# A two-block network on one core: the recurrence's preparation starts at the second product instead of the first, and activations move by 32 bytes

## The chip, the cores and the metric

The kernel runs on one core of one Trainium2 chip. The metric is the device time of one execution in microseconds. TensorE is called PE below, VectorE DVE, ScalarE ACT, GpSimd POOL and SyncE SP.

## The reference, cut to what matters

Two residual blocks of width 2048 run over 256 tokens. Each is a mixer followed by a sparse "peer" feed-forward layer, and everything is float32:

```python
# block 1
merged = gate_a * (o_a @ w_branch_a) + gate_b * (o_b @ w_branch_b)
x = x + merged @ w_out                                  # out_proj
x = x + peer(rmsnorm(x))                                # peer layer 1
...
# block 2: an mLSTM and an S5 recurrence in parallel, then
x = x + merged2 @ w_out_2
x = x + peer(rmsnorm(x))                                # peer layer 2

def peer(xb):            # 16384 experts, 8 heads x 16 chosen per token
...
    a = gelu(u_emb[expert] . xb)
    return sum((g * a) * v_emb[expert])

def s5_groups(u, lam_re, lam_im, log_dt, b_re, b_im, c_re, c_im, d, glu_w):
    dt = exp(log_dt);  mag = exp(lam_re * dt)
    ar = mag * cos(lam_im * dt);  ai = mag * sin(lam_im * dt)
...                                       # powers of ar + i*ai, b and c scaled by them
```

The part of S5 that depends on parameters alone (the powers, and the tables made from them) can be computed at any time before block 2. It is called S5's preparation below.

## The kernel before, in words

**Products.** A float32 product is made of three products of halves (`products`, matmul at L220): hi·hi, hi·lo and lo·hi. Weights come in tiles of 128x2048, in two parts `w_raw` of 128x1024, by DMAs from SP. For each part ACT writes `w_hi` (L205), and DVE (L211) or POOL (L209) writes `w_lo`. Each of these names has four buffers, so two tiles.

**The peer layer** does not gather experts. In each of two rounds (r = 0, 1) the first product `u` multiplies the tokens with 64 weight tiles (128x256 outputs, 48 matmuls per tile, operands `hT_hi` and `hT_lo`); Gelu and a gate follow, and the second product `v` uses 64 weight tiles again (512 columns, 24 matmuls a tile, operands `coef_hi` and `coef_lo`, made on ACT and DVE at L260).

**The gates of a round** are prepared in 32 groups of 8 tokens. For each group POOL and DVE make one-hot matrices `oh1` (L491; 6 of 8 on POOL in round 0, `G0 = 6`), DVE makes `oh`, `rh` and `rl` (L494 to L499), and PE multiplies them into `ps_g` (L505, L506).

**Order.** Work beside the main loop is written as generators ("lanes") in `K.bg`; `K.step(n)` runs them for n credits between weight tiles. The order inside each engine is then settled when the program is built: an instruction that is ready by the builder's own estimate may be placed ahead of earlier-written ones, unless `behind(x)` holds it until after x. Engines execute their own rows in order.

**S5's preparation** (`_s5_prepare`, L1094) is such a lane, run within peer layer 1. Its first part is about 215 small DVE instructions, mostly on 128x32, two Sin activations, and the table `base`. POOL then makes eight tables from `base` (L1194 to L1196, six instructions of 128x256 and two DMAs, L1201 and L1202, each). Then eight blocks follow (`expand`): DVE makes `s_work` (L1212 to L1219) in the buffer where `base` was, PE transposes it and multiplies (L1244, L1249: 192 matmuls in all), POOL expands a second table, and POOL's DMAs write both to DRAM.

**Addresses.** `hT()` allocates the two halves of the transposed activations. In the program's memory map they stand 32 bytes past a multiple of 64 bytes; weight parts and `coef` stand at a multiple of 64; the attention output `o` and the normalised `cqT` of block 1 also stand at a multiple of 64. So the two operands of a matmul differ by 32 bytes (modulo 64) wherever `hT` is used, and by 0 for `coef`, `o` and `cqT`. `out_proj` takes its activations in an `hT()` as well, with the weights as the moving operand (512 columns, 384 matmuls in each of the two blocks).

Of the kernel before, what the change touches and what calls it, by code (L numbers as in the profile page):

```python
# [7 lines left out]
F32, F32R, F16, U32, I32 = dt.float32, dt.float32r, dt.float16, dt.uint32, dt.int32  # L8
AF = mybir.ActivationFunctionType
OP = mybir.AluOpType  # L10
AX = mybir.AxisListType

P = 128
T = 256
TB = 2
D = 2048
KD = D // P
# [16 lines left out]
class Ctx:  # L34


    def __init__(self, ctx, tc):
        self.tc, self.nc = tc, tc.nc
        nc = self.nc
        pool = lambda name, bufs, **kw: ctx.enter_context(tc.tile_pool(name=name, bufs=bufs, **kw))  # L40
        self.const = pool("const", 1)
        self.small = pool("small", 1)
        self.state = pool("state", 1)
        self.wp = pool("weights", 2)
        self.pad = pool("pad", 1)
        self.two = pool("pairs", 2)
        self.pad3 = pool("pad3", 1, side="right")
        self.top = pool("hT", 1, side="right")
        for p, n in ((self.pad, 0), (self.pad3, 448)):
            if n:  # L50
                nc.gpsimd.memset(p.tile([P, n // 4], F32, name="pad"), 0.0)
        self.ps = pool("psum", 2, space=bass.MemoryType.PSUM)
        it = self.const.tile([P, P], F32, name="iota_f")
        nc.gpsimd.iota(it, pattern=[[1, P]], base=0, channel_multiplier=-1,
                       allow_small_or_imprecise_dtypes=True)
        self.diff = it
        self.ident = self.const.tile([P, P], F32, name="ident")
        nc.vector.tensor_scalar(self.ident, it, 0.0, None, op0=OP.is_equal)
        self.iota = self.const.tile([P, P], F16, name="iota_h")
        nc.gpsimd.iota(self.iota, pattern=[[1, P]], base=0, channel_multiplier=0,  # L60
                       allow_small_or_imprecise_dtypes=True)
        self.half_pi = self.const.tile([P, 1], F32, name="half_pi")
        nc.vector.memset(self.half_pi, float(np.pi / 2))
        self.x = self.state.tile([P, TB, D], F32, name="x")
        self.sq = self.small.tile([P, TB, 4], F32, name="x_sq")
        self.sq2 = self.small.tile([P, TB, 4], F32, name="x_sq2")
        self.twice, self.first, self.normed, self.done, self.fused = False, {}, {}, set(), {}
        self.bg = []
        self.late = []
        self.credit = 0.0  # L70
        self.fine = 0
        self.last = None

    def defer(self, fn):

# [75 lines left out]
    def step(self, n):  # L151
# [4 lines left out]
        while self.credit > 0 and idle < len(self.bg):  # L156
# [6 lines left out]
            self.credit -= took  # L163
            idle = 0 if took else idle + 1

    def lane(self):

        chain = []

        def run():  # L170
            while True:
                while not chain:
                    yield 0
                x = chain.pop(0)
                if x is None:
                    return
                yield from x

        self.bg.append(run())
        return chain  # L180
# [15 lines left out]
    def weights_now(self, src, n, pool):  # L196
        nc = self.nc
        self.fine -= 1
        h = n // 2
        raw, hi, lo = ([self.wp.tile([P, D // 2], d, name=nm, bufs=4)[:, :h] for _ in range(2)]  # L200
                       for nm, d in (("w_raw", F32), ("w_hi", F32R), ("w_lo", F32R)))
# [4 lines left out]
        for i in range(2):  # L206
            m = max(0, min(h, (2 - i) * h - pool))
            if m < h:
                nc.gpsimd.tensor_tensor(lo[i][:, m:], raw[i][:, m:], hi[i][:, m:].bitcast(F32), op=OP.subtract)  # L209
            if m:  # L210
                nc.vector.tensor_tensor(lo[i][:, :m], raw[i][:, :m], hi[i][:, :m].bitcast(F32), op=OP.subtract)  # L211
        return Halves(hi, h), Halves(lo, h)

    def products(self, items, left, half=None):
# [66 lines left out]
            self.last = v.scalar_tensor_tensor(r, q, 1.5, r, op0=OP.add, op1=OP.mult)  # L281
        return r

    def hT(self):
        return (self.top.tile([P, KD, T], F32R, name="hT_hi"),
                self.top.tile([P, KD, T], F32R, name="hT_lo"))

    def norm_T(self):

# [38 lines left out]
def peer(K, wq, keys, u, v, g_out, g_next=None, dst=None, later=None):  # L328
# [8 lines left out]
    nc, ctx = K.nc, ExitStack()  # L337
# [144 lines left out]
    TG = 8  # L482
    st = {}

    def gates(r, on_pool):

        def prepare(t0):
            oh1 = K.two.tile([P, TG, P], F16, name="oh1", tag="two_a", bufs=2)
            for t in range(TG):
                e = nc.gpsimd if t < on_pool else nc.vector  # L490
                e.tensor_scalar(oh1[:, t], K.iota, i1T[:, t0 + t:t0 + t + 1], None, op0=OP.is_equal)  # L491
            oh2 = rp.tile([P, TG, NJ], F16, name="oh2", bufs=2)
            b2 = lambda a: a[:, t0:t0 + TG, None].to_broadcast([P, TG, NJ])
            nc.vector.tensor_tensor(oh2, K.iota[:, None, r * NJ:(r + 1) * NJ].to_broadcast([P, TG, NJ]),  # L494
# [40 lines left out]
    for r in range(2):  # L535
        st.update(done=0, groups=0, A=[rp.tile([P, 16, T], F32, name="acts", tag="acts", bufs=4) for _ in range(4)])
        K.bg.append(gates(r, 8 if r else G0))
        for jp in range(NJ // 2):
            if r == 0 and st["groups"] == T // TG and later is not None:
                K.bg.append(later(rp))  # L540
                later = None
            ps = K.ps.tile([P, 2, T], F32, name="ps_u", bufs=2)
            for jj in range(2):
                if jp == NJ // 2 - 1 and jj:
# [13 lines left out]
            K.credit = 0.0  # L558
            K.step(1)
        if later is not None:  # L560
            K.bg.append(later(rp))
            later = None
        end = r == 1
        ext = {}
# [118 lines left out]
def mix1(K, I):  # L683
# [6 lines left out]
    ps_u = lambda shape: K.ps.tile(shape, F32, name="ps_u", bufs=2)  # L690
    ps_v = lambda shape: K.ps.tile(shape, F32, name="ps_v", bufs=4)

    grow = b8([P, D], "gain_row")[0:1]
    nc.sync.dma_start(grow, I["norm_mix_row"])
    ones = wt([P, T], "ones", 3, tag="one")[0:1, 0:P]
# [299 lines left out]
    for i in range(KD):  # L995
# [7 lines left out]
        nc.vector.tensor_tensor(m, m, ps[:, 0], op=OP.mult)  # L1003
        nc.vector.tensor_tensor(g1, g1, ps[:, 1], op=OP.mult)
        nc.vector.tensor_tensor(m, m, g1, op=OP.add)
    mh, ml = K.hT()
    for q in range(4):
        K.split(mh[:, 4 * q:4 * q + 4], ml[:, 4 * q:4 * q + 4], mg[:, 4 * q:4 * q + 4])
    out_proj(K, I["w_out"], mh, ml, K.gain(I["norm_ffn_g"], mp, "b8", 5))
# [266 lines left out]
def mix2(K, I, dram):  # L1276
# [332 lines left out]
    for h in range(MH):  # L1609
# [2 lines left out]
            conv(dst, in_cols(I["in2_qk"][4 * h + i]), 4 * h + i)  # L1612
            K.step(SQ)
        ready["h"] = h + 1
    ch, cl = K.hT()

    def before(i):
        while i >= 2 and have["ys"] < 4 * (i - 1):
# [178 lines left out]
```

## Time and profile before

| | |
|---|---|
| median of 3 runs | 4299.8 us (4299.35 to 4306.35) |
| the profiled execution | 4299.48 us, its span 4297.4 us |
| mean granted PE clock | 0.981 |
| PE busy | 4149.5 us, 97% of the span |
| DVE, ACT, POOL busy | 2831.5 us (66%), 2019.8 us (47%), 1535.1 us (36%) |

All times in the trace count from the span's start. Peer layer 1 runs its first product of round 0 from 690.6 to 1168.9 us, and its second from 1168.9 to 1543.6; the same loops of round 1 end at 1920.2 and 2268.3. Peer layer 2 has its first product of round 0 from 2808.0 to 3213.8 us. These bounds are first and last matmuls of each loop. The profiled execution lasts 2.1 us longer than its span, and is 0.3 us shorter than the median.

### The profile page before, as it was taken

The page shows a single profiled execution, that of the slowest core. Times are in us where ns is not written, and L with a number is a line of the kernel's source. Part 1 is how long each engine was busy: PE and PEld are TensorE (multiplying, and loading weights), DVE is VectorE, ACT ScalarE, POOL GpSimd, SP SyncE. Part 2 cuts the span into 40 slices and gives each one's busy share as a digit, 9 for nine tenths or more (in the row PEclk, how much of TensorE's full clock was granted, in tenths as well). Part 3 has the DMA queues.
Part 4 walks back from the last instruction along what each step waited for, and adds up shares of the span by engine and source line. Part 5 has one row for each costly group of instructions (what it writes and reads, how often), then busy time and mean ns, then how long its engine had stood idle before and what let it go on. Part 6 is the DMA issues. An engine that isn't in the chain of part 4 may idle for free. (4 is left out here: it accounts for less than half of the span.)

```text
span 4297.4 us, 74404 instructions
## 1 busy us (share of the span) xinstructions
PE 4149.5 (97%) x29233; PEld 3827.3 (89%) x29233; DVE 2831.5 (66%) x4666; ACT 2019.8 (47%) x2848; POOL 1535.1 (36%) x1318
## 2 busy tenths in 40 slices
PE   8999999888999999999998999999999999999999
PEld 7999989778888899998888998999998889999887
DVE  6775559887557656665556556798855556665565
ACT  5565443433344444445553455444445554444554
POOL 1100023789214147730005452369910006772000
PEclk9999999999999999999998999999999999999999
DMA  5445554454456655555666555545555555555555
GB/s 178 162 150 189 182 175 141 145 169 144 154 201 218 208 184 180 178 181 193 201 207 207 177 164 176 165 143 177 171 179 192 195 195 181 180 180 185 192 204 167
DMA packets 234160, 769.95 MB, mean 179 GB/s; under 512 B 44304, under 2 KB 46352, under 8 KB 233041
## 3 DMA queue, kind: packets, MB, share of 16 engines
q1 hardware_dynamic: 227906, 742.96, 52.5%
q0 software_dynamic: 5904, 22.25, 1.4%
q8 instruction: 229, 3.75, 0.3%
q14 instruction: 121, 0.99, 0.1%
HBM read 748.85 MB, written 16.25 MB: 178 GB/s over the span
## 5 line engine op out<-in xcount | busy, mean ns | idle before, releaser
L211 DVE TENSOR_TENSOR w_lo<-w_raw,w_hi 128x1024 fp32r<-128x1024 f32 (+3 forms) x1347 | 1631.8, 1244 | 1220.9 <-issue 941.6
L205 ACT CAST w_hi<-w_raw 128x1024 fp32r<-128x1024 f32 (+1 forms) x1388 | 1445.5, 1045 | 1603.9 <-PE ps_v L220 632.7
L220 PE MATMUL ps_u<-hT_hi,w_hi 128*128 128x256 f32 x5712 | 1404.0, 287 | 15.4 <-ACT acts L555 7.1
L220 PE MATMUL ps_u<-hT_lo,w_hi 128*128 128x256 f32 x5712 | 1387.1, 284 | 0.0
L491 POOL TENSOR_SCALAR oh<-iota_h,i1T 128x128 f16<-128x128 f16 x896 | 910.1, 1033 | 659.8 <-PE ps_v L220 492.7
L220 PEld LDWEIGHTS ps_u<-hT_hi,w_hi 128*128 128x128 f32 x5712 | 1098.6, 192 | 18.2 <-ACT acts L555 7.6
L220 PEld LDWEIGHTS ps_u<-hT_lo,w_hi 128*128 128x128 f32 x5712 | 1098.8, 192 | 1.9
L220 PE MATMUL ps_u<-hT_hi,w_lo 128*128 128x256 f32 x5712 | 739.2, 281 | 32.0 <-POOL w_lo L209 21.2
L220 PEld LDWEIGHTS ps_u<-hT_hi,w_lo 128*128 128x128 f32 x5712 | 699.8, 189 | 36.2 <-POOL w_lo L209 22.2
L220 PE MATMUL ps_v<-w_hi,coef_lo 128*128 128x512 f32 x2048 | 692.8, 390 | 2.4 <-DVE coef_lo L260 2.3
L220 PE MATMUL ps_v<-w_hi,coef_hi 128*128 128x512 f32 x2048 | 689.5, 390 | 0.0
L220 PE MATMUL ps_v<-w_lo,coef_hi 128*128 128x512 f32 x2048 | 512.5, 389 | 0.0
L220 PEld LDWEIGHTS ps_v<-w_hi,coef_lo 128*128 128x128 f32 x2048 | 383.1, 188 | 83.2 <-DVE coef_lo L260 4.4
L220 PEld LDWEIGHTS ps_v<-w_hi,coef_hi 128*128 128x128 f32 x2048 | 384.5, 188 | 79.7
L220 PEld LDWEIGHTS ps_v<-w_lo,coef_hi 128*128 128x128 f32 x2048 | 384.3, 188 | 79.6
L209 POOL TENSOR_TENSOR w_lo<-w_raw,w_hi 128x768 fp32r<-128x768 f32 (+3 forms) x159 | 310.1, 1957 | 353.3 <-PE ps_u L220 154.5
L259 ACT CAST coef_hi<-acts 128x512 fp32r<-128x512 f32 x256 | 159.4, 624 | 181.1 <-PE ps_v L220 177.8
L260 DVE TENSOR_TENSOR coef_lo<-acts,coef_hi 128x512 fp32r<-128x512 f32 x256 | 184.3, 721 | 6.0 <-ACT coef_hi L259 6.0
L119 POOL TENSOR_TENSOR normed<-x,gain 128x512 f32<-128x512 f32 x22 | 37.1, 1708 | 367.5 <-DVE x L96 280.1
L505 PE MATMUL ps_g<-rh,oh 128*128 128x64 f16 x1024 | 85.5, 197 | 40.8 <-POOL oh L491 35.5
L498 DVE TENSOR_TENSOR rh<-oh,g_hi 128x512 f16<-128x512 f16 x128 | 102.4, 800 | 19.8 <-PE ps_g L506 19.8
L515 ACT ACTIVATE acts<-ps_g 128x128 f32<-128x128 f32 (+7 forms) x318 | 60.6, 255 | 113.9 <-DVE acts L512 113.7
(490 smaller groups left out, 3573.2 us busy)
## 6 DMA issues: line engine op xcount, KB each, us to landing
w_raw<-in_p_u SPq DMA_DIRECT2D x512, 512.0 KB, 4.1
w_raw<-in_p_v SPq DMA_DIRECT2D x512, 512.0 KB, 4.3
w_raw<-in_in_gates SPq DMA_DIRECT2D x64, 512.0 KB, 4.0
w_raw<-in_w_out SPq DMA_DIRECT2D x64, 512.0 KB, 3.8
w_raw<-in_p_q SPq DMA_DIRECT2D x48, 512.0 KB, 4.1
w_raw<-in_in_t SPq DMA_DIRECT2D x38, 512.0 KB, 4.1
w_raw<-in_w_ab SPq DMA_DIRECT2D x32, 512.0 KB, 4.0
w_raw<-in_in_qk SPq DMA_DIRECT2D x32, 512.0 KB, 3.7
```

The source lines that it names most:

```text
L119: eng.tensor_tensor(self.normed_cols(tb, c), self.x[:, tb, cc], gb[:, cc], op=OP.mult)
L205: nc.scalar.copy(hi[i], raw[i])
L209: nc.gpsimd.tensor_tensor(lo[i][:, m:], raw[i][:, m:], hi[i][:, m:].bitcast(F32), op=OP.subtract)
L211: nc.vector.tensor_tensor(lo[i][:, :m], raw[i][:, :m], hi[i][:, :m].bitcast(F32), op=OP.subtract)
L220: self.last_mm = self.nc.tensor.matmul(out, lhsT=a, rhs=b, start=start, stop=stop)
L259: self.nc.scalar.copy(hi, src)
L260: return self.nc.vector.tensor_tensor(lo, src, hi.bitcast(F32), op=OP.subtract)
L491: e.tensor_scalar(oh1[:, t], K.iota, i1T[:, t0 + t:t0 + t + 1], None, op0=OP.is_equal)
L498: nc.vector.tensor_tensor(rh, oh2, b2(gh), op=OP.mult)
L505: nc.tensor.matmul(ps[:, t], lhsT=oh1[:, t], rhs=rh[:, t], start=True, stop=False)
L515: nc.scalar.activation(dst(nd, 16), src(nd, 16), AF.Copy, scale=1.0 / GS)
```

## The change

S5's preparation was appended to the lanes in the first product of round 0, as soon as the gates' groups were done being issued. It is now appended when that loop is over, just ahead of the second product, wrapped in `pin`: each of its steps is held behind the last `w_lo` instruction on DVE (`K.lo[0]`) and the last `w_lo` or one-hot on POOL (`K.lo[1]`).

Besides, `hT` is now one tile for both halves, by default shifted by 8 floats; the two calls ahead of `out_proj` ask for a shift of 0. A `pad` tile of 32 bytes at the start of block 1's pool moves that block's tiles, `o` and `cqT` among them, by 32 bytes. So matmuls of `out_proj` go from 32 bytes of difference to 0 (768 of 512 columns), those of `o` and `cqT` from 0 to 32 (768 and 144 of 256 columns); 72 matmuls of block 1's `ckvT` go from 32 to 0. The `u` and `v` products of the peer layers stay as they were.

```diff
@@ Ctx
+        self.lo = [None, None]
...
+    def pin(self, lane):
+        while True:
+            with self.behind(self.lo[0]), self.behind(self.lo[1]):
+                took = next(lane, None)
+            if took is None:
+                return
+            yield took
@@ weights_now
-                nc.gpsimd.tensor_tensor(lo[i][:, m:], raw[i][:, m:], hi[i][:, m:].bitcast(F32), op=OP.subtract)
+                self.lo[1] = nc.gpsimd.tensor_tensor(lo[i][:, m:], raw[i][:, m:], hi[i][:, m:].bitcast(F32), op=OP.subtract)
...
-                nc.vector.tensor_tensor(lo[i][:, :m], raw[i][:, :m], hi[i][:, :m].bitcast(F32), op=OP.subtract)
+                self.lo[0] = nc.vector.tensor_tensor(lo[i][:, :m], raw[i][:, :m], hi[i][:, :m].bitcast(F32), op=OP.subtract)
@@ hT
-    def hT(self):
-        return (self.top.tile([P, KD, T], F32R, name="hT_hi"),
-                self.top.tile([P, KD, T], F32R, name="hT_lo"))
+    def hT(self, shift=8):
+
+        both = self.top.tile([P, 2 * KD * T + 8], F32R, name="hT")[:, shift:shift + 2 * KD * T]
+        both = both.rearrange("p (two k t) -> p two k t", two=2, k=KD)
+        return both[:, 0], both[:, 1]
@@ gates, prepare
+                if t < on_pool:
+                    K.lo[1] = one
@@ peer, the loop over the first product
-            if r == 0 and st["groups"] == T // TG and later is not None:
-                K.bg.append(later(rp))
-                later = None
@@ peer, behind that loop
         if later is not None:
-            K.bg.append(later(rp))
+            K.bg.append(K.pin(later(rp)))
             later = None
@@ mix1
+    nc.gpsimd.memset(wt([P, 8], "pad", 1), 0.0)
...
-    mh, ml = K.hT()
+    mh, ml = K.hT(0)
@@ mix2
-    ch, cl = K.hT()
+    ch, cl = K.hT(0)
```

Outside of the first and second product of round 0 in peer layer 1, each engine has the same instructions in the same order before and after.

**On POOL**, in the first product of round 0, the order before has S5's tables (`s_work`, `s_prm`, `s_tab`) between the one-hots `oh` of one group and of the next:

```order
76 L491 TENSOR_SCALAR oh_10247<-iota_h,i1T 128x128 x6
77 L1196 TENSOR_TENSOR s_work<-s_work,s_prm 128x256
78 L1194 TENSOR_TENSOR s_work<-s_work 128x256 x2
79 L1195 TENSOR_TENSOR s_prm<-s_work 128x256
80 L491 TENSOR_SCALAR oh_10348<-iota_h,i1T 128x128 x6
81 L1196 TENSOR_TENSOR s_work<-s_work,s_prm 128x256
82 L1201 DMA s_tab<-s_work 128x512
83 L491 TENSOR_SCALAR oh_10444<-iota_h,i1T 128x128 x6
```

After the change (where L491 has become L500, and S5's lines are 9 further down) all one-hots of the round stand first, and S5's rows follow the last group of them:

```order
73 L500 TENSOR_SCALAR oh_11985<-iota_h,i1T 128x128 x6
74 L500 TENSOR_SCALAR oh_12086<-iota_h,i1T 128x128 x6
75 L500 TENSOR_SCALAR oh_12183<-iota_h,i1T 128x128 x6
76 L1109 DMA s_prm<-in_s_lam 128x96
77 L1239 DMA s_bc<-in_s_bc 128x512 x2
78 L1211 DMA s_tab<-s_decay 128x256 x2
79 L1222 TENSOR_TENSOR s_prm<-s_bc,s_prm 128x512
80 L1203 TENSOR_TENSOR s_work<-s_work 128x256 x2
81 L1204 TENSOR_TENSOR s_prm<-s_work 128x256
```

The whole of S5 on POOL has moved behind the gates of round 0; the gates of round 1 stand behind it.

**On DVE**, in the same loop, the order before has S5's small instructions (`s_prm`, L1141 to L1168) between the `w_lo` of two weight tiles and in front of `rh`, which PE's gate products read:

```order
888 L1161 TENSOR_TENSOR s_prm<-s_prm 128x32
889 L1164 TENSOR_TENSOR s_prm<-s_prm 128x32
890 L1163 TENSOR_TENSOR s_prm<-s_prm 128x32
891 L1165 TENSOR_TENSOR s_prm<-s_prm 128x32
892 L1166 TENSOR_SCALAR s_prm<-s_prm 128x32
893 L211 TENSOR_TENSOR w_lo<-w_raw,w_hi 128x1024
894 L1167 TENSOR_TENSOR s_prm<-s_prm 128x32
895 L1168 TENSOR_TENSOR s_prm<-s_prm 128x32
896 L211 TENSOR_TENSOR w_lo<-w_raw,w_hi 128x256
```

After the change (`w_lo` is at L218, `coef_lo` at L267) DVE's rows in that loop are the same without S5's. They stand in the second product instead; these rows are the end of its densest tile, which has 24 of them between two `coef_lo` (L1168 to L1177 and L1191 are S5's, the latter on `base`):

```order
1143 L218 TENSOR_TENSOR w_lo<-w_raw,w_hi 128x1024
1144 L1176 TENSOR_TENSOR s_prm<-s_prm 128x32
1145 L1177 TENSOR_TENSOR s_prm<-s_prm 128x32
1146 L218 TENSOR_TENSOR w_lo<-w_raw,w_hi 128x1024
1147 L1207 COPY s_decay<-s_prm 128x256
1148 L1169 TENSOR_TENSOR s_prm<-s_prm 128x32
1149 L1191 TENSOR_TENSOR s_prm<-s_work,s_prm 128x128
1150 L1168 TENSOR_TENSOR s_prm<-s_prm 128x32
1151 L1171 SCALAR_TENSOR_TENSOR s_prm<-s_prm 128x32
1152 L1191 TENSOR_TENSOR s_prm<-s_work,s_prm 128x128
1153 L267 TENSOR_TENSOR coef_lo<-acts,coef_hi 128x512
```

**On DVE, ten tiles further on**, the first `expand` (L1221) stands between the weight parts of a tile and its `coef_lo`. It writes the buffer from which POOL makes the tables:

```order
1197 L218 TENSOR_TENSOR w_lo<-w_raw,w_hi 128x1024 x2
1198 L267 TENSOR_TENSOR coef_lo<-acts,coef_hi 128x512
1199 L218 TENSOR_TENSOR w_lo<-w_raw,w_hi 128x1024 x2
1200 L1207 COPY s_decay<-s_prm 128x256
1201 L267 TENSOR_TENSOR coef_lo<-acts,coef_hi 128x512
1202 L1208 MEMSET s_decay 128x4
1203 L218 TENSOR_TENSOR w_lo<-w_raw,w_hi 128x1024 x2
1204 L1221 TENSOR_TENSOR s_work<-s_bc,s_prm 128x4x128
1205 L267 TENSOR_TENSOR coef_lo<-acts,coef_hi 128x512
```

From the last instruction on `base` to this row DVE has nine pairs of `w_lo`, so nine tiles of the second product. PE's 192 matmuls of S5 lie within the second product of round 0 before and after (before from its third tile on, now from about its 26th to its 61st of 64).

## Rows read from the trace of the kernel before

**Rows 1.** The page, busy time by engine, over the span.
```profile
PE 4149.5 (97%) x29233; PEld 3827.3 (89%) x29233; DVE 2831.5 (66%) x4666; ACT 2019.8 (47%) x2848; POOL 1535.1 (36%) x1318
```

**Rows 2.** Windows, matmuls of L220 alone: length, PE, PEld, clock, DMA share, GB/s.
```profile
690.60:1168.90 478.30, 390.10 (x3023) 380.25 (x3024) 0.92 0.45 150
2808.00:3213.80 405.80, 376.87 (x3068) 369.59 (x3068) 0.97 0.51 167
...
1168.90:1543.60 374.70, 357.62 (x1538) 285.80 (x1537) 1.00 0.62 206
1920.20:2268.30 348.10, 348.10 (x1538) 288.17 (x1536) 1.00 0.59 197
```

**Rows 3.** Windows, all instructions: length, PE, PEld, DVE, ACT, POOL, clock, DMA, GB/s.
```profile
808.00:900.00 92.00, 78.97 (x692) 76.43 (x690) 85.42 (x279) 38.79 (x67) 66.50 (x61) 0.96 0.48 157
900.00:1110.00 210.00, 172.80 (x1557) 167.19 (x1558) 160.57 (x272) 68.17 (x124) 192.60 (x202) 0.89 0.44 146
...
2920.00:3130.00 210.00, 210.00 (x2090) 208.93 (x2090) 171.11 (x290) 95.51 (x175) 196.86 (x177) 1.00 0.54 179
...
1250.00:1467.00 217.00, 214.62 (x1027) 178.01 (x1026) 156.55 (x159) 103.74 (x121) 75.50 (x69) 1.00 0.65 215
```

**Rows 4.** Waits of PE from 808 to 1168: total us, times, longest.
```profile
PE ps_g L505 <- POOL oh L491: 33.7, 36, 5.9
```

**Rows 5.** Groups on POOL, 808 to 1110: count | busy us, mean ns | idle before.
```profile
L491 POOL TENSOR_SCALAR oh<-iota_h,i1T 128x128 f16<-128x128 f16 x172 | 166.3, 982 | 1.9 <-PE ps_g L506 1.7
...
L1196 POOL TENSOR_TENSOR s_work<-s_work,s_prm 128x256 f32<-128x256 f32 x16 | 17.7, 1104 | 0.6
L1194 POOL TENSOR_TENSOR s_work<-s_work 128x256 f32<-128x256 f32 x16 | 15.3, 976 | 0.8 <-DVE s_work L1183 0.8
L1195 POOL TENSOR_TENSOR s_prm<-s_work 128x256 f32<-128x256 f32 x16 | 13.5, 846 | 0.4
L1201 POOL DMA_DIRECT2D s_tab<-s_work x8 | 4.8, 603 | 1.2 <-POOL s_work L1196 1.2
L1202 POOL DMA_DIRECT2D s_tab<-s_decay x8 | 4.5, 564 | 10.7 <-DVE s_prm L1143 4.7 <-DVE s_prm L1163 3.1 <-DVE s_prm L1144 2.9
```

**Rows 6.** Groups on DVE, 808 to 900, two of S5's.
```profile
L1159 DVE TENSOR_TENSOR s_prm<-s_prm 128x32 f32<-128x32 f32 x7 | 4.1, 580 | 0.0
...
L1161 DVE TENSOR_TENSOR s_prm<-s_prm 128x32 f32<-128x32 f32 x7 | 1.4, 194 | 0.0
```

**Rows 7.** Timeline of DVE: start, us, instruction.
```profile
853.47 0.18 DVE L1153 TENSOR_TENSOR s_prm<-s_prm 128x32 f32<-128x32 f32 x1
853.57 0.18 DVE L1143 TENSOR_TENSOR s_prm<-s_prm 128x32 f32<-128x32 f32 x1
```

**Rows 8.** Groups on DVE, 1180 to 1250 (second product, POOL idle).
```profile
L211 DVE TENSOR_TENSOR w_lo<-w_raw,w_hi 128x1024 fp32r<-128x1024 f32 x26 | 30.7, 1223 | 33.9 <-issue 33.9
L260 DVE TENSOR_TENSOR coef_lo<-acts,coef_hi 128x512 fp32r<-128x512 f32 x13 | 8.9, 685 | 0.0
```

**Rows 9.** Groups on DVE, 1250 to 1450 (second product, POOL on S5).
```profile
L211 DVE TENSOR_TENSOR w_lo<-w_raw,w_hi 128x1024 fp32r<-128x1024 f32 x65 | 87.7, 1380 | 47.7 <-issue 39.0 <-ACT w_hi L205 8.7
L260 DVE TENSOR_TENSOR coef_lo<-acts,coef_hi 128x512 fp32r<-128x512 f32 x32 | 28.2, 882 | 0.0
```

**Rows 10.** Windows, matmuls of L220: inside out_proj of block 1, inside a second product.
```profile
534.00:619.00 85.00, 85.00 (x366) 68.44 (x365) 1.00 0.54 181
2000.00:2085.00 85.00, 85.00 (x377) 70.41 (x376) 1.00 0.58 191
```

**Rows 11.** Timeline of PE: 16 matmuls of `o`, the first, and what follows them.
```profile
353.94 0.28 PE L220 MATMUL ps_v<-o_hi,w_hi 128*128 128x256 f32 x1
...
355.86 1.12 PE L220 MATMUL ps_v<-o_hi,w_lo 128*128 128x256 f32 x8
```

**Rows 12.** Timeline of PE in a first product: ten matmuls of `hT`, likewise.
```profile
1699.74 0.28 PE L220 MATMUL ps_u<-hT_hi,w_hi 128*128 128x256 f32 x1
...
1700.90 2.03 PE L220 MATMUL ps_u<-hT_hi,w_lo 128*128 128x256 f32 x16
```

More of the change, by code (lines that the diff above doesn't have):

```diff
@@ L44, in __init__ @@
         self.wp = pool("weights", 2)
-        self.pad = pool("pad", 1)
         self.two = pool("pairs", 2)
@@ L48, in __init__ @@
         self.top = pool("hT", 1, side="right")
-        for p, n in ((self.pad, 0), (self.pad3, 448)):
-            if n:
-                nc.gpsimd.memset(p.tile([P, n // 4], F32, name="pad"), 0.0)
+        nc.gpsimd.memset(self.pad3.tile([P, 112], F32, name="pad"), 0.0)
         self.ps = pool("psum", 2, space=bass.MemoryType.PSUM)
@@ L490, in prepare @@
                 e = nc.gpsimd if t < on_pool else nc.vector
-                e.tensor_scalar(oh1[:, t], K.iota, i1T[:, t0 + t:t0 + t + 1], None, op0=OP.is_equal)
+                one = e.tensor_scalar(oh1[:, t], K.iota, i1T[:, t0 + t:t0 + t + 1], None, op0=OP.is_equal)
+                if t < on_pool:
+                    K.lo[1] = one
             oh2 = rp.tile([P, TG, NJ], F16, name="oh2", bufs=2)
```

## The prediction

> **What bounds the kernel now.** The page's first part comes first: PE is busy for 4149.5 of 4297.4 us [rows 1], so a change can gain only where PE idles or runs slower than it could. The windows by loop show where that is. The first product of round 0 takes 478.30 us in peer layer 1 and 405.80 us in peer layer 2, although the two do the same matmuls; its clock is 0.92 and 0.97 [rows 2]. The reader should see that the only difference between these two loops in the program is S5's preparation, which stands in the first of them. The second product of round 0 of layer 1 takes 374.70 us against 348.10 us in round 1 [rows 2]; there the difference is S5's 192 matmuls and what surrounds them.
>
> The windows by stretch show where in the first loop the time goes. From 808, when S5's first DVE instruction runs, to 1110, when the gates are done, PE is busy for 78.97 of 92 and 172.80 of 210 us, the second at a clock of 0.89; POOL is busy for 192.60 of the 210 [rows 3]. In the corresponding stretch of layer 2 PE is busy for all of 210 us, at clock 1.00, with POOL at 196.86 [rows 3]. So POOL is nearly full in both, but in layer 1 a part of what fills it is S5's. The chain of waits of PE agrees: 36 waits, 33.7 us together, for POOL's one-hots [rows 4].
>
> **The change part by part.**
>
> *First product of round 0.* All of S5 leaves it, on DVE and on POOL (the order shows S5's tables gone from between the one-hots), and nothing is added. What is left is layer 2's loop. Up to 808 the two loops have the same rows, so I take the whole difference: 478.30 - 405.80 = 72.5 us [rows 2]. A second way gives nearly the same. At layer 2's rate of 2090 matmuls in 210 us, 0.1005 us each, layer 1's 692 + 1557 matmuls of the two stretches would take 226 us, and they took 302 [rows 3]: 76 us. The lower bound is PE's idle time in these stretches without anything for the clock, 13.0 + 37.2 = 50 us [rows 3]; the upper is the 76 us with some 2 us for the waits of the tail, 78. I take 72.5, since it is read from the very loop that is left.
>
> *Second product of round 0, DVE.* PE's part of S5 lies in this loop already, and its cost of 374.70 - 348.10 = 26.6 us [rows 2] stays. New is the chain of about 215 small DVE instructions, in tiles 0 to 14 mostly. A tile takes PE 348.10 / 64 = 5.44 us [rows 2], DVE needs 2 x 1.223 + 0.685 = 3.13 us of it [rows 8], so 2.3 us are free per tile. A small instruction starts 0.10 us after the one before where nothing disturbs it [rows 7]; some had a mean of 580 ns in the first product, others 194 [rows 6]. While the chain runs POOL is idle in the new place (the one-hots are done, the tables wait for `base`), so I take 0.10 to 0.19, with 0.15 in the middle: 215 x 0.15 = 32 us, against 14 x 2.3 = 32 us of free time. That is level on the mean; the densest tile has 24 of them, 3.6 us, so 1.3 us too much, and DVE's lead over PE, a tile at most because of four buffers, levels some of it. I put this at 2 us. The bounds: 0 if DVE's lead covers it; if every instruction cost the mean of 580 and 194, 0.39 us, the chain would take 84 us against the 24 x 2.3 = 55 us that are free up to the first `expand`, so 29 us.
>
> *Second product, the wait for the tables.* The first `expand` on DVE overwrites `base`, so it waits until POOL has read `base` for the last of its eight tables. Those cost 2 x (1.104 + 0.976 + 0.846) + 0.603 + 0.564 = 7.0 us each [rows 5], 56 us together. DVE comes to that row nine tiles after `base` is complete, 9 x 5.44 = 49 us. It stands there for about 7 us, and behind it on DVE is `coef_lo` of the next tile, which PE reads. What PE sees is the 7 us and the 1.1 us of the row itself less a part of the free time; afterwards DVE regains its lead in 2 or 3 tiles. I take 6 us; 0 if POOL is quicker without one-hots beside it (the duration in these rows is one beside a DVE that is 76% busy [rows 3]), 14 if POOL's rows become a tenth slower.
>
> *Second product, slower neighbours.* With POOL on S5, `w_lo` took 1380 instead of 1223 ns and `coef_lo` 882 instead of 685 [rows 8, 9], so 0.5 us a tile, inside the 2.3. ACT, which makes the two Sin activations, was busy for 103.74 of 217 us there [rows 3]. Together 1 us, bounds 0 and 3. The tables' 16 DMAs are POOL's and stand in the 56 us. The one-hots of round 1 stand behind S5 on POOL, but they need buffers that the second product gives up at its end, and S5 on PE is through by its 61st tile: nothing.
>
> `pin` adds waits only for rows that stand behind DVE's `w_lo` anyway; on POOL nothing but S5 is queued behind them until round 1, and no DMA of SP's is moved.
>
> The sum of the second product is 2 + 6 + 1 = 9 us, between 0 and 29 + 14 + 3 = 46.
>
> *Addresses.* In `out_proj` 366 matmuls took 85 us, 232.2 ns each, in a second product 377 took 85 us, 225.5 ns; both have 512 columns, clock 1.00 and PE busy throughout [rows 10]. They differ in the distance of the two operands, 32 against 0. If that is the cause, 768 x 6.7 ns = 5.2 us are gained. For 256 columns it goes the other way round: 16 matmuls of `o` at distance 0 took 1.92 us, 120 ns each [rows 11], ten of `hT` at 32 took 1.16 us, 116 ns [rows 12]. The 768 + 144 matmuls that go from 0 to 32 would gain up to 912 x 4 ns = 3.6 us; I take 2.3, as the `o` products are mixed with others. Together 7.5 us, bounds 0 and 8.8.
>
> The Trainium skill, page "SBUF — State Buffer", sections "SBUF: two separate sides" and "Who interferes with whom", gives PE two independent read ports and says that it never waits on anyone; by it an offset between operands changes nothing and this term would be 0. The trace does not agree, with 232.2 against 225.5 ns; what the page doesn't speak of is two reads of PE itself.
>
> **Sum.** 4299.5 - 72.5 + 9 - 7.5 = 4228.5 us, against the profiled execution's own time, which is 0.3 us under the median of the runs. I say 4229.
>
> **The rivals.**
>
> *The preparation's waits come along.* The small instructions cost 0.39 us in the second product too, 29 us instead of 2, so it loses 36 us. For it speaks the slow half of the small instructions [rows 6] and that the free time on DVE is only just enough; against it that POOL had 192.60 us of work in 210 there [rows 3] and has none during the chain here. 4299.5 - 72.5 + 36 - 7.5 = 4255.5 us.
> The Trainium skill, same page, section "Who interferes with whom", states an exclusive lock between a DVE instruction with two SBUF inputs and a GpSimd instruction that reads SBUF. By that the slow small instructions were blocked by one-hots, and would be quick beside an idle POOL; the trace's 580 and 194 ns agree.
>
> *The one-hots stay the bound.* POOL is at 196.86 of 210 us in layer 2 too [rows 3]; a little more jitter in layer 1 and only the idle time's 50 us is gained: 4299.5 - 50 + 9 - 7.5 = 4251 us. Against it: layer 2 runs its loop with the same rows without a loss.
>
> *Addresses are worth nothing.* The 6.7 ns come from something else that the two shapes don't share, such as which operand is the activations: 4299.5 - 72.5 + 9 = 4236 us.
>
> *Slower than before.* The place is the first `expand`: DVE stands until POOL's tables are made, and all of `w_lo` and `coef_lo` stands behind it. To end over 8.6 us slower, the second product must lose 72.5 + 7.5 + 8.6 = 89 us more than now. With 3 us for the two other terms this wait must be 86 us, so the tables must take 49 + 86 = 135 us instead of 56, 2.4 times the rows. That would take POOL blocked by DVE for more than half of the time; beside a DVE at 76% it took 56. In that case: 4299.5 - 72.5 - 7.5 + 89 = 4308.5 us or more.
>
> That S5 doesn't move, the order excludes.
>
> **How the numbers follow.** The forecast has 0.57, the preparation's waits 0.18, the one-hots 0.06, addresses worth nothing 0.12, slower 0.04; 0.03 are left for a loss that just eats the gain. The range takes in the first four cases and the bounds of the terms on the good side (78 and 8.8 us gained, nothing lost: 4213 us); on the other it ends a little above the waits' 4255.5, since two terms have still higher bounds: 4210 to 4260 us. A measurement of this kernel tells about 0.2%, 8.6 us, from no change. So faster has 0.93, the same 0.03, slower 0.04.
>
> **What would show it.** In the changed kernel's windows the first product of round 0 should last about 406 us, with its clock at 0.97 and PE fully busy once S5 would have begun; PE's waits for one-hots should fall from 33.7 us to a few. The second product should last about 384 us, with one stretch of a few us near its 24th tile where DVE's first `expand` waits for POOL. `out_proj` should run at 226 ns a matmul in both blocks, and `o` at about 117. All other loops should be unchanged. The prediction is wrong if DVE is short in the second product's first 14 tiles, if POOL's tables take much more than 56 us, or if the first product keeps waits that layer 2's doesn't have.

## The result, and the profile after

The changed kernel takes 4248.75 us (median of 4 runs, 4247.59 to 4252.32) against 4299.58 for the kernel before beside it: a ratio of 0.988, 95% interval 0.9863 to 0.9897. It is 50.8 us faster; 70.5 were forecast. The time lies in the range. The profiled execution has a span of 4250.6 us, 46.8 less than before, and in it the loops can be compared one by one. It is the slowest of the four, 3.6 us above their median.

The windows by loop after the change, matmuls of the weights' products alone, which now stand at L227 (length, PE, PEld, clock, DMA share, GB/s): first and second product of round 0, second product of round 1, and layer 2's first product of round 0.

```profile
685.20:1092.20 407.00, 371.35 (x3023) 363.67 (x3024) 0.96 0.50 165
1092.20:1501.30 409.10, 367.90 (x1538) 294.13 (x1538) 0.96 0.61 199
1877.90:2226.10 348.20, 348.20 (x1539) 288.20 (x1537) 1.00 0.59 197
2761.10:3166.90 405.80, 376.25 (x3058) 368.86 (x3057) 0.97 0.51 167
```

Against [rows 2], the first product fell from 478.3 to 407.0 us, 71.3 less, to a microsecond of layer 2's 405.8. The second product rose from 374.7 to 409.1 us, 34.4 more, where 9 were forecast. All the rest of the program gave 10 us. Some 5 of that is the address part, shown below; the other 5 is no effect that could be shown: the stretch from layer 1's last product to layer 2's first, 6 us shorter here, took between 533 and 542 us in the twelve executions profiled.

PE's waits in the first product, from 803 us to its end (total us, times, longest), are down from 33.7 us [rows 4]:

```profile
PE ps_g L516 <- POOL oh L500: 2.7, 4, 1.3
```

The windows of the second product (length, PE, PEld, DVE, ACT, POOL, clock, DMA share, GB/s) show that its loss is not spread evenly:

```profile
1092.20:1200.00 107.80, 107.80 (x478) 89.25 (x478) 93.14 (x260) 55.72 (x63) 25.21 (x26) 1.00 0.61 201
1200.00:1260.00 60.00, 50.96 (x220) 41.46 (x219) 39.93 (x38) 22.97 (x26) 47.64 (x53) 0.91 0.58 195
1260.00:1501.30 241.30, 225.75 (x1037) 186.21 (x1035) 160.25 (x163) 103.37 (x121) 84.03 (x80) 0.96 0.61 200
```

In the first 108 us, which hold DVE's chain of small instructions, PE never idles. What is lost is lost from 1200 us on, and DVE's waits in the loop name the places (total us, times, longest):

```profile
DVE s_work L1221 <- DMA s_w<-s_work: 23.0, 4, 7.4
DVE w_lo L218 <- ACT w_hi L212: 13.9, 4, 4.4
DVE s_work L1225 <- POOL s_prm L1204: 8.4, 1, 8.4
...
DVE s_decay L1207 <- DMA s_tab<-s_decay: 5.4, 2, 5.0
```

The third row is the wait of the first `expand` for POOL's tables that the prediction worked out. The first and the fourth it did not have. The fourth is DVE's wait until the decay rows of an earlier table have been written. The first is the wait of a later `expand` until the DMA has written the block before it to DRAM, out of the same buffer. The kernel before had it too, but small; this is the corresponding row of its second product, from 1168 to 1545 us:

```profile
DVE s_work L1212 <- DMA s_w<-s_work: 5.8, 5, 1.7
```

What such a wait costs PE is seen in its timeline (start, us, instruction, idle before and who ended it), at the first `expand`:

```profile
1232.48 1.07 PE L227 MATMUL ps_v<-w_hi,coef_hi 128*128 128x512 f32 x4
1240.27 2.07 PE L227 MATMUL ps_v<-w_hi,coef_lo 128*128 128x512 f32 x4 [6.71 <-DVE coef_lo L267]
1242.14 0.63 PE L227 MATMUL ps_v<-w_hi,coef_hi 128*128 128x512 f32 x1
1242.57 0.63 PE L227 MATMUL ps_v<-w_hi,coef_lo 128*128 128x512 f32 x1
```

PE idles 6.7 us, and then a matmul follows the one before after 0.43 us instead of 0.227. The windows of these stretches give the clock (columns as above):

```profile
1240.20:1244.00 3.80, 3.73 (x9) 2.96 (x10) 3.77 (x5) 1.05 (x1) 2.37 (x2) 0.51 0.26 78
1244.00:1250.00 6.00, 6.00 (x31) 5.00 (x30) 6.00 (x5) 2.34 (x3) 5.84 (x4) 1.00 0.54 169
```

For 3.8 us the granted clock is 0.51, which is the 1.2 GHz level, and then full again. Adding up what the gaps between starts exceed 0.227 us by, over the whole loop, gives 25.6 us in gaps over 0.6 us, in which PE stood (2.3 in the kernel before), and 11.6 us in 54 gaps of 0.36 to 0.6 us, most of them 0.43, the pace at half the clock (0.6 in 2 before). So of 34 us more, some 23 are idle time and some 11 are the clock after it.

### The profile page after: what moved, and what is told of

Its sections match the earlier page's. It is cut to its first block, busy times and chain, and to the rows that moved or that the text cites. A ratio compares the mean times of both kernels' runs of the same rounds, so it can differ in the third digit from the quotient of the medians.

```text
span 4250.6 us, 74415 instructions
## 1 busy us (share of the span) xinstructions
PE 4127.9 (97%) x29233; PEld 3813.8 (90%) x29233; DVE 2824.9 (66%) x4666; ACT 2017.1 (47%) x2846; POOL 1559.2 (37%) x1319
## 5 line engine op out<-in xcount | busy, mean ns | idle before, releaser
L218 DVE TENSOR_TENSOR w_lo<-w_raw,w_hi 128x1024 fp32r<-128x1024 f32 (+3 forms) x1347 | 1644.6, 1253 | 1193.0 <-issue 877.8
L227 PE MATMUL ps_u<-hT,w_hi 128*128 128x256 f32 x11424 | 1439.3, 283 | 4.6 <-ACT acts L563 2.7
L227 PEld LDWEIGHTS ps_u<-hT,w_hi 128*128 128x128 f32 x11424 | 1381.3, 190 | 8.2 <-ACT acts L563 3.0
L500 POOL TENSOR_SCALAR oh<-iota_h,i1T 128x128 f16<-128x128 f16 x896 | 927.9, 1053 | 611.7 <-PE ps_v L227 433.6
L227 PE MATMUL ps_u<-hT,w_lo 128*128 128x256 f32 x5712 | 738.5, 281 | 33.4 <-POOL w_lo L216 21.6
L227 PEld LDWEIGHTS ps_u<-hT,w_lo 128*128 128x128 f32 x5712 | 700.2, 189 | 36.3 <-POOL w_lo L216 22.3
L227 PE MATMUL ps_v<-w_hi,coef_lo 128*128 128x512 f32 x2048 | 699.1, 394 | 20.8 <-DVE coef_lo L267 18.4
L227 PE MATMUL ps_v<-w_hi,coef_hi 128*128 128x512 f32 x2048 | 692.1, 392 | 0.0
L227 PE MATMUL ps_v<-w_lo,coef_hi 128*128 128x512 f32 x2048 | 513.8, 390 | 0.0
L227 PEld LDWEIGHTS ps_v<-w_hi,coef_lo 128*128 128x128 f32 x2048 | 388.2, 190 | 103.6 <-DVE coef_lo L267 20.6
L227 PEld LDWEIGHTS ps_v<-w_hi,coef_hi 128*128 128x128 f32 x2048 | 387.0, 189 | 80.6
L227 PEld LDWEIGHTS ps_v<-w_lo,coef_hi 128*128 128x128 f32 x2048 | 385.2, 188 | 80.4
L267 DVE TENSOR_TENSOR coef_lo<-acts,coef_hi 128x512 fp32r<-128x512 f32 x256 | 187.7, 734 | 5.5 <-ACT coef_hi L266 5.5
L227 PE MATMUL ps_v<-w_hi,hT 128*128 128x512 f32 (+2 forms) x576 | 125.2, 367 | 1.5 <-ACT hT L266 1.1
L227 PEld LDWEIGHTS ps_v<-w_hi,hT 128*128 128x128 f32 x576 | 100.0, 188 | 20.4 <-ACT hT L266 1.3
L505 DVE TENSOR_TENSOR oh<-iota_h,i2T 128x512 f16<-128x512 f16 x128 | 92.2, 721 | 2.9
```

What stands on the lines that cost most here:

```text
L218: self.lo[0] = nc.vector.tensor_tensor(lo[i][:, :m], raw[i][:, :m], hi[i][:, :m].bitcast(F32), op=OP.subtract)
L227: self.last_mm = self.nc.tensor.matmul(out, lhsT=a, rhs=b, start=start, stop=stop)
L267: return self.nc.vector.tensor_tensor(lo, src, hi.bitcast(F32), op=OP.subtract)
L500: one = e.tensor_scalar(oh1[:, t], K.iota, i1T[:, t0 + t:t0 + t + 1], None, op0=OP.is_equal)
```

## The experiments

The kernel before was run again beside these runs; its medians were 4298.2 to 4299.6 us, so their times can be set side by side.

**One part alone.** e1 is the kernel before with the address part, e2 the changed kernel without it:

```diff
# e1, on the kernel before (with the hT of the changed kernel)
+    nc.gpsimd.memset(wt([P, 8], "pad", 1), 0.0)
-    mh, ml = K.hT()
+    mh, ml = K.hT(0)
-    ch, cl = K.hT()
+    ch, cl = K.hT(0)
# e2 takes these lines back in the changed kernel
```

> The kernel before with the address part alone; every engine keeps its order. If the distance of a matmul's two operands sets its cadence, out_proj goes from 233 to 227 ns a matmul, the products of o from 120 to about 117, and the time falls by 5 to 8 us, to about 4293. If the distance changes nothing, the time stays at 4299.6 within 2 us.

> The changed kernel without the address part; its order is that of the changed kernel. If the two parts simply add, the time is that of the changed kernel plus 5 to 8 us, about 4255; the first product of round 0 takes about 407 us and the second about 409. If the addresses are worth nothing, it is 4249.

e1 took 4293.7 us against 4298.2, ratio 0.999 (0.9981 to 0.9999); e2 took 4253.4, ratio 0.9902 (0.9887 to 0.9917), so 4.6 more than the changed kernel's 4248.75. By e1 the addresses are worth 4.5 us, with an interval from 0.4 to 8.2; e2's six runs lie between 4243.6 and 4264.8, so its 4.6 agrees but shows little by itself. The late start is worth 45 to 46 us. By the first and last matmuls of each stage, `out_proj` took 86.9 us in e1 and 89.4 in the kernel before, in block 2 92.9 and 95.2, and the stage with `o` 173.7 and 177.1: together 8.2 us. Part of it is given back at one place near the start, where `cqT` is used (windows of e1, columns as in the last windows above):

```profile
87.00:91.00 4.00, 1.14 (x11) 0.94 (x9) 1.30 (x2) 3.67 (x10) 0.00 (x0) 0.89 0.36 133
91.00:97.30 6.30, 6.30 (x31) 6.30 (x32) 1.79 (x2) 2.92 (x5) 0.00 (x0) 0.53 0.25 92
```

PE idles 2.86 us there in e1 and 2.71 in the kernel before. For the next 6.3 us the clock is 0.53 in e1; in the kernel before it stays at 1.00. That the quicker matmuls of `cqT` bring this about is not shown. The same 200 matmuls around it took 32.6 us instead of 30.0 in e1, and 31.4 in the changed kernel. In e2 the first product took 406 us as in the changed kernel, and the second 400.5 in the execution profiled: with the very same order this loop differs by 8 us between executions.

**The addresses, turned the other way.** e5 shifts `coef` to a distance of 32, e6 puts `hT` at a distance of 0 everywhere:

```diff
# e5, on the changed kernel
-                ch = K.two.tile([P, 2, T], F32R, name="coef_hi", tag="two_a", bufs=2)
-                cl = K.two.tile([P, 2, T], F32R, name="coef_lo", tag="two_b", bufs=2)
+                ch, cl = (K.two.tile([P, 2 * T + 16], F32R, name=n, tag=t, bufs=2)[:, 8:8 + 2 * T]
+                          .rearrange("p (j t) -> p j t", j=2) for n, t in (("coef_hi", "two_a"), ("coef_lo", "two_b")))
# e6, on the changed kernel
-    def hT(self, shift=8):
+    def hT(self, shift=0):
```

> The changed kernel with coef_hi and coef_lo 32 bytes past a multiple of 64, so that the 6144 matmuls of 512 columns of the second products go from a distance of 0 to 32; every engine keeps its order. If the distance sets the cadence, they go from 226.6 to 233 ns, as out_proj had at 32, and the time rises by 6144 x 6.7 ns = 41 us, to about 4290; some of it may hide where PE waits in round 0. If out_proj's gain had another cause, the time stays at 4249.

> The changed kernel with hT at a distance of 0 everywhere; every engine keeps its order. If 256 columns prefer 32, as o and cqT showed, 17136 matmuls go from 116.6 to 120 ns and the time rises by 17136 x 3.4 ns = 58 us, to about 4305, less what PE's waits in the first products of round 0 hide. If 0 is better for every shape, the time falls; if the distance does nothing for 256 columns, it stays at 4249.

e5 took 4280.7 us, 32 more than the changed kernel, and e6 4290.9, 42 more (ratios to the kernel before 0.9967, 0.9954 to 0.998, and 0.9977, 0.9968 to 0.9987). Both are slower than the changed kernel, so 512 columns go faster at 0 and 256 columns faster at 32. The window of e5's second product of round 1:

```profile
1877.10:2234.40 357.30, 357.30 (x1538) 288.51 (x1536) 1.00 0.57 192
```

A loop without a wait, PE busy throughout at full clock, takes 357.3 instead of 348.2 us, 6 ns more for each of its 1536 matmuls (232.6 instead of 226.7). In e6 it is the first product of round 1 that takes 386.1 us, against 376.4 in the changed kernel, 3.2 ns for each of 3072. The first row below is e6's window, the second the changed kernel's:

```profile
1511.60:1897.70 386.10, 375.88 (x3073) 370.18 (x3073) 1.00 0.53 175
```

```profile
1501.50:1877.90 376.40, 366.20 (x3073) 360.60 (x3072) 1.00 0.54 180
```

The totals are 9 and 16 us under the expected 41 and 58: the effects per matmul are 6 and 3.2 ns, not 6.7 and 3.4, and where PE waits for others most is hidden (the second product of round 0 in layer 1 took 408 us in e5, as in the changed kernel; the first products of the two rounds 0 rose by some 1 and 3 us in e6, not by 9.7).

In all these runs the weights stay at a multiple of 64 and the activations are moved, so no run tells the distance of the two operands from the activations' own place. The 512 columns are the weights', as the moving operand, and the 256 columns mostly the activations'; this could be what turns the sign. But some matmuls of `hT` have 256 columns with the weights as the moving operand. Their starts are 118.3 ns apart in the changed kernel and 119.8 in e6 (means over some 340 pairs of neighbours): they too go faster at 32, if by half as much. So the sign goes with the number of columns.

**The DMA out of the table buffer.** e3 issues it from ACT:

```diff
-        g.dma_start(dram["w1"][i], W[:, 0])
+        nc.scalar.dma_start(dram["w1"][i], W[:, 0])
```

> The changed kernel, with the DMA that writes DVE's table of a block to DRAM issued from ACT, behind ACT's own copies, instead of from POOL. Theory: in the changed kernel it is issued 13 us late, because POOL's queue has the next block's load and four POOL instructions in front of it, and DVE's next expand waits for its landing, 23 us in all. Then these waits go and the second product of round 0 falls from 409 to about 385 us, the whole to about 4225. Rival: the landing itself is slow among the weights' transfers, or DVE has too much to do; then it stays at 400 us or more and the whole above 4240.

It took 4239.1 us, ratio 0.9864 (0.985 to 0.9879): 9.7 less than the changed kernel, where the theory said 24. The loop fell from 409.1 to 395.8 us. DVE's waits in it:

```profile
DVE s_work L1225 <- POOL s_prm L1204: 8.5, 1, 8.5
DVE s_work L1221 <- DMA s_w<-s_work: 7.3, 3, 2.7
DVE s_decay L1207 <- DMA s_tab<-s_decay: 7.2, 2, 4.7
```

The wait for this DMA fell from 23.0 to 7.3 us and the other two stayed. In e2, e5 and e6, which keep the changed kernel's order, it was 19.9, 16.2 and 21.2 us, so the fall is more than executions differ by, and the place in POOL's queue was a real part of the wait. But the loop did not come down to 385. With the DMA early, DVE's `expand` of one block falls together with POOL's of the next, and both run slowly (timeline of DVE in e3; alone such an instruction takes 0.69 us):

```profile
1301.88 1.57 DVE L1221 TENSOR_TENSOR s_work<-s_bc,s_prm 128x512 f32<-128x512 f32 x1
1303.37 1.79 DVE L1222 TENSOR_TENSOR s_prm<-s_bc,s_prm 128x512 f32<-128x512 f32 x1
1305.08 1.56 DVE L1225 TENSOR_TENSOR s_work<-s_bc,s_prm 128x512 f32<-128x512 f32 x1
```

The tile of PE's matmuls in which this falls took 4.9 us over the undisturbed 5.44. That is about half of what is missing; the rest is spread over the loop.

**Which part of S5 cost the first product its 72 us.** e4 lets DVE's chain start in the first product again; `s5_late` becomes true behind that loop, and only the tables and what follows wait for it:

```diff
...
-            with self.behind(self.lo[0]), self.behind(self.lo[1]):
+            with self.behind(self.lo[0] if self.s5_late else None), self.behind(self.lo[1] if self.s5_late else None):
...
+            if r == 0 and st["groups"] == T // TG and later is not None:
+                K.bg.append(K.pin(later(rp)))
+                later = None
...
+        K.s5_late = True
...
+    while not K.s5_late:
+        yield 0
     for i in range(8):
```

> The changed kernel, but DVE's chain of small instructions starts in the first product of round 0 as before the change; POOL's tables and all that follows stay behind that loop. Theory: what cost 72 us there were POOL's rows between the one-hots, so the first product takes some 410 us and the whole about 4250. Rival: the chain on DVE, in front of the operands of the gates' products, cost the part from 808 to 900, some 22 us; then the first product takes about 428 us and the whole about 4270.

It took 4249.3 us, ratio 0.9888 (0.9873 to 0.9902), as much as the changed kernel. Windows of its first and second product:

```profile
684.50:1099.40 414.90, 374.69 (x3023) 365.80 (x3024) 0.96 0.48 162
1099.40:1497.10 397.70, 363.25 (x1538) 290.16 (x1537) 0.98 0.60 205
```

The start of the chain, 175 of 226 of S5's rows on DVE, costs the first product 7.9 us. So about 64 of its 71 us come from POOL's S5 rows, or from the last quarter of the chain, which e4's order puts into the second product; the rival's 22 us for the chain are not there. PE's waits in the first product speak for POOL's rows, since with most of the chain in it those for one-hots are as short as in the changed kernel:

```profile
PE ps_g L517 <- POOL oh L501: 2.7, 4, 1.3
```

The second product took 11 us less than in the changed kernel, which made good the 8 us. This can't be told from chance: in the four executions with the changed kernel's order (its own, e2, e5 and e6) that loop took 400.5 to 410.5 us.

**Sharing the tables.** e7 is e3 with tables 2 and 5 made on DVE and the decay rows' DMAs issued from ACT:

```diff
+        e = v if i in (2, 5) else g
...
-            g.tensor_tensor(tab[:, part], big(part), fine(0), op=OP.mult)
+            e.tensor_tensor(tab[:, part], big(part), fine(0), op=OP.mult)
...
-        g.dma_start(dram["tab"][i, :, 512:768], dk.rearrange("p b c -> p (b c)"))
+        nc.scalar.dma_start(dram["tab"][i, :, 512:768], dk.rearrange("p b c -> p (b c)"))
```

> The kernel of e3 with two of the eight tables made on DVE instead of POOL and the DMAs of the decay rows issued from ACT. Theory: two more waits of the second product of round 0 go, that of the first expand for POOL's tables (8.5 us, PE lost 8.8) and that for the decay rows' DMA (PE lost 5.4); then this loop falls from 396 to some 384 us and the whole from 4239 to about 4227. Rival: DVE's two tables cost what they save; then it stays at 4239.

It took 4231.9 us, ratio 0.984 (0.9826 to 0.9853), 7 less than e3 where 12 were expected; the loop took 390.0 us, not 384. The waits for the tables and the decay rows are gone from DVE's list, but a new one of 4.4 us for the tables' own DMA stands there, and in three tiles PE still lost 3.5 to 5 us each beyond S5's own matmuls.

**The blocks in another loop.** e8 is e3 with the blocks held until the second product of round 1, e9 is e8 with the DMA back on POOL:

```diff
...
         end = r == 1
+        K.s5_go = end
...
+    while not K.s5_go:
+        yield 0
     ahead = inputs(0)
# e9, on e8
-        nc.scalar.dma_start(dram["w1"][i], W[:, 0])
+        g.dma_start(dram["w1"][i], W[:, 0])
```

> The kernel of e3 with the eight blocks held until the second product of round 1; the chain and the tables stay in that of round 0. Theory: no expand waits for the tables any more, and PE's 25 us for S5's matmuls move to round 1 unchanged; round 0's second product falls from 396 to about 356 us (348, the decay wait and 2), round 1's rises from 348 to about 380, together 8 us less: about 4231. Rival: the blocks meet the layer's end in round 1 (norm and gains on DVE and POOL) and cost there what they save: 4239 or more.

> The kernel of e8 with that DMA back on POOL. Theory: its place in POOL's queue makes DVE wait in each block, with or without the tables ahead; then round 1's second product takes about 395 us and the whole about 4241. Rival: the waits of the changed kernel came from the backlog that the tables left on POOL; then round 1's second product takes about 380 us as in e8, and the whole is about 4226.

e8 took 4225.95 us, ratio 0.9824 (0.9811 to 0.9837), and e9 4221.6, ratio 0.982 (0.9804 to 0.9837); the two can't be told apart, and they beat the changed kernel by 23 and 27 us. Windows of the second products of rounds 0 and 1 in e8, and then in e9:

```profile
1090.40:1438.50 348.10, 348.10 (x1538) 288.32 (x1537) 1.00 0.61 202
1815.20:2195.40 380.20, 356.44 (x1537) 285.99 (x1536) 1.00 0.61 206
```

```profile
1088.10:1436.10 348.00, 348.00 (x1538) 288.12 (x1537) 1.00 0.59 202
1812.80:2191.40 378.60, 355.74 (x1538) 286.11 (x1536) 1.00 0.61 207
```

With the chain and the tables alone, round 0's second product takes 348 us, not one more than a loop without S5 and 8 less than expected, since DVE's wait for the decay rows no longer reaches PE. The blocks cost round 1 some 30 to 32 us, against 26.6 us in the kernel before. In e9 DVE still waits for the DMA on POOL, but 9.1 us instead of 23.0 (its waits in round 1):

```profile
DVE s_work L1223 <- DMA s_w<-s_work: 9.1, 3, 4.9
```

The theory's 395 us for e9 were wrong: the place in POOL's queue is not enough to make 23 us. Nor does the backlog that the tables left on POOL, the rival's cause, account for most of it. In the changed kernel POOL stood idle for 18.9 us up to 1297.9, waiting for PE, so that the backlog was gone by then, and three of the four waits, 15.6 of the 23.0 us, came later. These rows show one of them, the issue on POOL and the `expand` that waited:

```profile
1335.69 0.59 POOL L1267 DMA_DIRECT2D s_w<-s_work  x1
1341.53 0.69 DVE L1221 TENSOR_TENSOR s_work<-s_bc,s_prm 128x512 f32<-128x512 f32 x1 [4.70 <-DMA s_w<-s_work]
```

These are the same rows in the kernel before:

```profile
1296.55 0.59 POOL L1258 DMA_DIRECT2D s_w<-s_work  x1
1300.33 1.10 DVE L1212 TENSOR_TENSOR s_work<-s_bc,s_prm 128x512 f32<-128x512 f32 x1 [0.61 <-DMA s_w<-s_work]
```

From issue to landing it took 5.8 us in the first pair and 3.8 in the second. All four waits of the changed kernel had landings of 5.8 to 6.6 us; its two landings of 3.1 and 3.6 us had no wait, nor had two of its longer ones. In e9 the landings of the first six blocks took 3.2 to 3.5 us in four cases, and the longest wait, 4.9 us, had the longest, 6.0. In e3 six of eight still took 5.3 to 7.0 us, but from an earlier issue. So the stall went with two things together, a late issue and a long landing: e3 took away the one and e9 most of the other.

**Without the pin.**

```diff
-            K.bg.append(K.pin(later(rp)))
+            K.bg.append(later(rp))
```

> The changed kernel with the preparation appended ahead of the second product, but not held behind the parts of the weights. By its order the builder places S5's chain, tables and first expand back into the first product of round 0, so the first product takes about 478 us again and the whole about 4292, the time of the kernel before less the address part. If the place in the program's text were what counts, it would take about 4249.

It took 4289.3 us, ratio 0.998 (0.997 to 0.999). Its first product (window):

```profile
685.50:1166.30 480.80, 388.98 (x3024) 379.22 (x3025) 0.92 0.44 149
```

That is the 478 us of [rows 2] again, and 226 of S5's rows on DVE and 83 on POOL lie in this loop, as many as in the kernel before: written later but not held, the preparation goes back to where it was.

## Why the prediction was right, and where it was off

The measured 4248.75 us lies in the range, but as a number it is nearer to 4251 of the rival with the one-hots and to 4255.5 of the one with the preparation's waits than to 4229. What rules those two out is the windows and waits below. The second product's 34.4 us, too, lie within the 0 to 46 that its terms were given, but some 26 of them come from waits for which no term stood. That these bounds held is luck.

*First product of round 0*: right in mechanism and size, 71.3 us against 72.5. The loop that is left behaves as the same loop of layer 2, which was the whole argument; the rival in which the one-hots stay the bound fell with PE's 2.7 us of waits for them. e4 gives the reason a finer edge: the chain's start is worth 8 us, and POOL's rows, with the chain's last quarter, the rest.

*Second product, DVE's chain*: 2 us forecast, 0 measured. The small instruction that had a mean of 580 ns in [rows 6] stands at L1168 now, and took its undisturbed time (DVE's groups from 1092 to 1170):

```profile
L1168 DVE TENSOR_TENSOR s_prm<-s_prm 128x32 f32<-128x32 f32 x7 | 1.3, 184 | 0.0
```

Of the prediction's "slow half" a reading has to be put right: in [rows 6], six of the seven instructions behind the mean of 580 ns took 0.18 to 0.32 us, and one took 2.82, beside POOL (timeline of the kernel before):

```profile
872.11 2.82 DVE L1159 TENSOR_TENSOR s_prm<-s_prm 128x32 f32<-128x32 f32 x1
```

From 808 to 1110 in the kernel before, 16 of the 63 such instructions of S5 that began while POOL ran one of its own took over 0.3 us, and none of the 84 others. In the new place POOL's rows of S5 begin at 1166.8 us, behind most of the chain. The rival that took them to be slow there too fell with their undisturbed time; e8 and e9 show that chain and tables together can be hidden completely, when no block follows them. The Trainium skill's rule of an exclusive lock between DVE and GpSimd (page "SBUF — State Buffer", section "Who interferes with whom") said that they would be quick beside an idle POOL, and the trace agrees with 184 ns; so do e3's 1.6 us instead of 0.69 for DVE's `expand` beside POOL's.

*Second product, the wait for the tables*: 6 us forecast, 8.7 measured as the longer tile. POOL's instructions for the tables took 57 us, as worked out from [rows 5], but POOL also stood 6.9 us waiting for its own DMAs out of the two halves of the table buffer. These groups from 1160 to 1245 us show it:

```profile
L1205 POOL TENSOR_TENSOR s_work<-s_work,s_prm 128x256 f32<-128x256 f32 x16 | 19.9, 1243 | 0.6
L1204 POOL TENSOR_TENSOR s_prm<-s_work 128x256 f32<-128x256 f32 x16 | 15.1, 946 | 0.6
L1203 POOL TENSOR_TENSOR s_work<-s_work 128x256 f32<-128x256 f32 x16 | 13.0, 832 | 6.9 <-DMA s_tab<-s_work 6.9
```

*Second product, slower neighbours*: 1 us forecast. No tile of the loop outside those with S5's matmuls or with a wait named here took more than 0.2 us over its 5.44.

*The step that failed* is the sentence that S5's part on PE "lies in this loop already, and its cost of 374.70 - 348.10 = 26.6 us [rows 2] stays". That was taken for a cost of PE's matmuls alone, but it held the whole of the eight blocks: a ring from PE's transposes over POOL's queue and a DMA to DVE's next `expand`. In the kernel before DVE reached that row when the DMA had just landed (5.8 us of waiting, 1.7 at most), and nothing in the prediction asked how much room this ring had. After the change four `expand`s waited 23.0 us together, and PE lost 27 us in the four tiles, some 22 more than S5's matmuls and the same tiles' waits before account for. A second, smaller omission is the wait for the decay rows' DMAs, which stand behind the tables on POOL: 4.2 us of PE. The sum by these tiles is 22 + 8.7 + 4.2 = 35 us, against 34.4 measured; each item contains the half-clock stretch behind its idle time, which the prediction left out too. These are the sizes of one execution: in e2's, with the same order, the loop lost 25.8 us.

*Addresses*: 7.5 us forecast, 4.5 measured by e1, with an interval from 0.4 to 8.2. The rival that they are worth nothing fell with e1, e5 and e6. The terms themselves came out at 8.2 us, and a place where PE idles and the clock falls took back 1 to 3. The Trainium skill's statement that PE never waits on anyone (same page, section "SBUF: two separate sides") would have given 0; e5's 357.3 against 348.2 us in a loop with PE busy throughout shows that the place of an operand of PE itself changes its pace.

Why the landing of that DMA took from 3.1 to 7.5 us in the changed kernel stays open. In the stretch of the wait shown above the DMA engines were busier than in that of the kernel before (their windows, columns as above), which fits a meeting with the weights' transfers, but no run sets that alone:

```profile
1335.00:1342.00 7.00, 5.32 (x24) 4.08 (x22) 2.30 (x2) 2.73 (x3) 4.64 (x5) 1.00 0.84 277
1296.00:1301.00 5.00, 5.00 (x23) 4.14 (x23) 4.39 (x3) 2.58 (x3) 4.79 (x4) 1.00 0.72 243
```

## What to carry to other kernels

When work is moved into a loop, look not only at the free time of its engines but at every ring that already runs there, over a queue and a DMA back to an engine that the bound engine needs: measure how late its slowest link is now. Here a ring whose data landed just as they were needed, with waits of 1.7 us at most, became a stall of 4.7 to 7.4 us on four of eight turns. Work that is independent of other work in the same lane can go to different loops; here the chain and tables were free in one loop and the blocks cost 31 to 32 us in another (e8, e9), which was 23 to 27 us better than both in one. And moving a line in the program's text moves nothing where the order is settled again when the program is built (e10): look at the order that comes out.

## What the hardware showed unexpectedly

The same matmul ran at a different pace by where its activations stood modulo 64 bytes, with the weights at a multiple of 64: for 512 columns 226.7 ns at 0 and about 233 at 32, but for 256 columns 120 at 0 and 117 at 32. The sign goes with the number of columns; why is not explained by any run.

After some idle times of PE its clock was at the 1.2 GHz level: 0.51 for 3.8 us behind 6.7 us, and 0.53 for 6.3 us behind 2.86 us, in the windows above. Behind 2.71 us in the kernel before it stayed at 1.00. In the changed kernel's second product the clock cost 11.6 us beside 25.6 us of idle time.
